# Gate and up by rows with seven block products in place of eight for part of the depth, in a two-layer trunk on one core

## The chip, the core and the metric

One Trainium2 chip, of which one core runs the program. The metric is the device time of one execution in microseconds, the median of the runs. All inputs lie in HBM when it starts, and the output is written back there.

## What is computed

Two layers on 256 tokens of width 2048, in float32. A layer is a norm, one projection that feeds eight retention heads and a gated linear recurrence, an output projection added to x, and then the part that is changed:

```
D_MODEL = 2048
SEQ = 256
DEPTH = 2
D_FF = ((8 * D_MODEL // 3 + 255) // 256) * 256
...
        x = x + mix @ w_out[l]
        h = _rmsnorm(x, norm2_g[l])
        x = x + (jax.nn.silu(h @ ffn_w_gate[l]) * (h @ ffn_w_up[l])) @ ffn_w_down[l]
    return _rmsnorm(x, final_g)
```

D_FF is 5632, which is 44 chunks of 128 columns; D_MODEL is 16 chunks.

## The kernel before, in words

Every large product is made to float32 accuracy from three products of a shorter type: a weight w is split into hi (a copy in that type, by ScalarE) and lo = w - hi (by VectorE), an activation likewise (`pair`, L122 to L134), and hi*hi, hi*lo and lo*hi are summed in PSUM.

The work is a list of units. A unit is one block of weights of up to 128x2048, which SP fetches in one DMA (`load`, L544), which is split in two halves (`split`, L568 and L569) and then used by up to four blocks of matmuls. Three raw buffers and three pairs of hi and lo buffers rotate. The main loop (L648 to L663) writes the program block by block: ahead of a unit's first and third block stands the split of half of the unit after the next; behind each block, a counter of ticks releases small pieces of other work that were put off by so many blocks. The order of the instructions on each engine comes from that loop and from a scheduler that may move them a little.

Almost all units are column units (`column_unit`, L182): the weights are stationary, the tokens move. For each of the 16 chunks of the depth, L195 multiplies the hi weights with 512 columns (256 tokens hi, 256 tokens lo), and L198 the lo weights with 256 columns. The result has features on partitions and tokens in the free dimension. Only the v part of the projection (L441 to L443) has the tokens stationary and 512 weight columns moving, three matmuls for each chunk and each half of the tokens.

The feed-forward stage of a layer goes in three parts (`THIRDS`, 15, 15 and 14 chunks of D_FF). In each, every chunk f has a gate unit and an up unit (L512 and L513), with `gate` (L501) and `up` (L506) behind them: the two halves of the PSUM tile are joined (L178, L179), scaled by the row norm of the tokens, silu is taken (L505), gate and up are multiplied (L510) and split (L126, L127). Then 16 down units add to x (L406, L407). There are 88 gate and up units in a layer, 176 in all.

Of the kernel before, what the change touches and what calls it, by code (L numbers as in the profile page):

```python
# [26 lines left out]
THIRDS = [(0, 15), (15, 15), (30, 14)]  # L27
RAW = 3
WARM = 12
# [41 lines left out]
class Unit:  # L71


    def __init__(self, src, width, blocks, done=None, begin=None):
        self.src, self.width, self.blocks = src, width, blocks
        self.done, self.begin = done, begin
        self.split_at = (0, 2)
# [3 lines left out]
def trunk(ctx: ExitStack, tc, a, out):  # L81
# [4 lines left out]
    hi_p = pool("whi", 3)  # L86
    lo_p = pool("wlo", 3)
# [3 lines left out]
    big_ps = pool("big", 4, space=bass.MemoryType.PSUM)  # L91
    sm_ps = pool("sm", 4, space=bass.MemoryType.PSUM)
# [7 lines left out]

    def small():
        return sm_ps.tile([P, 512], F32, tag="sm", name="sm_ps")
# [78 lines left out]

    def column_unit(src, n_k, operand, done, begin=None, order=None):  # L182

        u = Unit(src, n_k * P, [], begin=begin)
        order = order or list(range(n_k))

        def block(i):
            ks = order[i : i + 4]

            def run():  # L190
                if i == 0:
                    u.ps = big_ps.tile([P, 512], F32, tag="big", name="acc_ps")
                for pr in (ks[:2], ks[2:]):
                    for k in pr:
                        PE.matmul(u.ps, lhsT=u.hi[:, k * P : (k + 1) * P],  # L195
                                  rhs=operand(k).rearrange("p a t -> p (a t)"), start=k == order[0], stop=False)
                    for k in pr:
                        PE.matmul(u.ps[:, T : 2 * T], lhsT=u.lo[:, k * P : (k + 1) * P], rhs=operand(k)[:, 0, :],  # L198
                                  start=False, stop=k == order[-1])
            return run  # L200

        u.blocks += [block(i) for i in range(0, n_k, 4)]
        u.done = lambda: done(u.ps)
        return u


    def rotary(ps, name):
        z = joined_halves(ps)
        t, u, o = tmp("rt"), tmp("ru"), tmp(name)
# [7 lines left out]
    def head(l, h):  # L217
# [86 lines left out]
    def lru(l, n):  # L304
# [68 lines left out]
        def y_done(ps):  # L373
            z = joined_halves(ps)
            y = one_p.tile([P, T], F32, tag=f"gy{n}", name="y")
# [33 lines left out]
    def after_residual(k, nxt, gains):  # L409
# [3 lines left out]
        if k == KD - 1:  # L413
            tk.after(2, lambda: sums([st["xa"]], D, "rs"))
            tk.after(4, lambda: rows("rs"))
# [7 lines left out]
    def v_units(l):  # L423

        res = []
        for g in range(2):
            hold = {}
            for s in range(4):
                u = Unit(a["w_v"][l, g, s], 2048, [])

                def block(kk, u=u, s=s, hold=hold):
                    def run():
                        k = s * 4 + kk
                        if k == 0:
                            hold["ps"] = [big_ps.tile([P, 512], F32, tag="big", name="v_ps") for _ in range(2)]
                        w = slice(kk * 512, (kk + 1) * 512)
                        x2 = st["h1", k]
                        for j in range(2):
                            t = slice(j * P, (j + 1) * P)
                            ps = hold["ps"][j]  # L440
                            PE.matmul(ps, lhsT=x2[:, 0, t], rhs=u.hi[:, w], start=k == 0, stop=False)  # L441
                            PE.matmul(ps, lhsT=x2[:, 0, t], rhs=u.lo[:, w], start=False, stop=False)  # L442
                            PE.matmul(ps, lhsT=x2[:, 1, t], rhs=u.hi[:, w], start=False, stop=k == KD - 1)  # L443
# [11 lines left out]
                u.blocks = [block(kk) for kk in range(4)]  # L455
# [7 lines left out]
    def layer_units(l):  # L463
# [17 lines left out]
        for n in range(KD):  # L481
# [3 lines left out]
            u = column_unit(a["w_out"][l, n], KD, lambda k: st["mix", l, k], done, order=order)  # L485
            if n == 0:
                rest, first_done = u.blocks.pop(), u.done
                u.done = None
            if n == 1:
                def held(rest=rest, first_done=first_done):  # L490
                    rest()
                    first_done()
                u.blocks.insert(3, held)
                u.split_at = (4, 4)
            res.append(u)


        for t, (f0, nf) in enumerate(THIRDS):
            for f in range(f0, f0 + nf):
                c = {}  # L500
                def gate(ps, c=c):  # L501
                    z = joined_halves(ps)
                    c["g"] = tmp("sg")
                    V.tensor_tensor(out=z, in0=z, in1=st["rs"], op=ALU.mult)  # L504
                    S.activation(out=c["g"], in_=z, func=AF.Silu)  # L505
                def up(ps, c=c, f=f):  # L506
                    z = joined_halves(ps)
                    m = tmp("mix")
                    V.tensor_tensor(out=c["g"], in0=c["g"], in1=st["rs"], op=ALU.mult)  # L509
                    V.tensor_tensor(out=m, in0=z, in1=c["g"], op=ALU.mult)  # L510
                    st["act", f] = pair(m)
                res.append(column_unit(a["w_gate"][l, f], KD, lambda k: st["h2", k], gate))  # L512
                res.append(column_unit(a["w_up"][l, f], KD, lambda k: st["h2", k], up))  # L513
            for n in range(KD):
# [7 lines left out]
                res.append(column_unit(a[f"w_down{t}"][l, n], nf, lambda k, f0=f0: st["act", f0 + k], done))  # L522
        return res

# [19 lines left out]
    def load(n):  # L544
        if n < len(units):
            u = units[n]
            u.raw = raw_p.tile([P, 2048], F32, tag="raw", name="raw")
            pieces = 4 if n < 4 else 1
            for q in range(pieces):
                w = slice(q * u.width // pieces, (q + 1) * u.width // pieces)  # L550
                nc.sync.dma_start(out=u.raw[:, w], in_=u.src[:, w])
                if n == 0:
                    nc.sync.dma_start(out=X[:, q, :], in_=a["x"][:, q])
# [193 lines left out]
```

## Time and profile before

| | |
|---|---|
| median of 3 runs | 2257.55 us (2257.39 to 2257.93) |
| the profiled execution | 2257.48 us, its span 2255.7 us |
| busy share | PE 99%, VectorE (DVE) 67%, ScalarE (ACT) 50%, GpSimd 3% |
| moved by DMA | 422.92 MB, mean 187 GB/s |

The span runs from the first to the last instruction that the profiler saw; the profiled execution's own time is 1.8 us more. A busy share says how much of the span an engine had work in flight. For TensorE it says little about speed, since matmuls overlap: there the time from one start to the next counts.

### The profile page before, as it was taken

What the parts mean: (1) busy time and instruction counts of PE and PEld (TensorE: products, weight loads), DVE (VectorE), ACT (ScalarE), POOL (GpSimd) and SP (SyncE); (2) the same over time, 40 slices, a digit from 0 to 9 for tenths busy, and PEclk for the clock granted to TensorE, in tenths of its full rate; (3) what the DMA queues carried; (4) which work ended last, traced back from release to release, by engine and by line L of the source; (5) the groups of instructions that cost most, each with busy time, mean ns of one, the idle gap of its engine ahead of it and who ended that gap; (6) DMA issues with size and microseconds to landing.
All of it is one profiled execution on the core that took longest, in us unless ns stands there. A gap on an engine that the chain in (4) does not pass through costs nothing.

```text
span 2255.7 us, 31764 instructions
## 1 busy us (share of the span) xinstructions
PE 2239.1 (99%) x12760; PEld 1949.4 (86%) x12760; DVE 1512.5 (67%) x2405; ACT 1127.1 (50%) x1648; POOL 59.8 (3%) x97
## 2 busy tenths in 40 slices
PE   9999999999999999999999999999999999999997
PEld 7888888888888888888888888888888888888886
DVE  6888876666566655666748889766665666556665
ACT  6667544544344443444546665444443444334453
POOL 0010100000000000000000101000000000000000
PEclk9999999999999999999999999999999999999999
DMA  7555555555555555555555554555555555555553
GB/s 286 183 186 181 172 195 191 183 191 189 184 200 187 186 186 189 188 190 179 201 193 179 180 197 165 189 182 192 191 183 195 188 187 184 192 188 190 193 175 112
DMA packets 63140, 422.92 MB, mean 187 GB/s; under 512 B 7312, under 2 KB 7952, under 8 KB 24592
## 3 DMA queue, kind: packets, MB, share of 16 engines
q1 hardware_dynamic: 60912, 414.60, 52.5%
q0 software_dynamic: 1792, 5.24, 0.8%
q8 instruction: 100, 1.64, 0.3%
q10 hardware_dynamic: 288, 1.05, 0.1%
q14 instruction: 48, 0.39, 0.0%
HBM read 418.77 MB, written 2.10 MB: 187 GB/s over the span
## 4 chain that ended last, share of the span: by engine, by line
PE 97%; DVE 1%; issue 0%; DMA 0%; POOL 0%; ACT 0%; SPq 0%; DVEq 0%; POOLq 0%
PE acc_ps L195 62%; PE acc_ps L198 31%; PE v_ps L442 1%; PE v_ps L443 1%; PE v_ps L441 1%; PE sm_ps L331 1%; DVE wlo L569 0%; PE sm_ps L240 0%; DMA raw<-in_w_v_dram 0%; DVE op L130 0%; PE sm_ps L289 0%; PE sm_ps L157 0%; PE sm_ps L241 0%; PE sm_ps L256 0%; PE sm_ps L255 0%
## 5 line engine op out<-in xcount | busy, mean ns | idle before, releaser
L195 PE MATMUL acc_ps<-op,whi 128*128 128x512 f32 x6016 | 1899.8, 397 | 0.0
L198 PEld LDWEIGHTS acc_ps<-op,wlo 128*128 128x128 f32 x6016 | 1129.8, 188 | 263.4
L569 DVE TENSOR_TENSOR wlo<-raw,whi 128x1024 fp32r<-128x1024 f32 (+3 forms) x808 | 950.0, 1187 | 366.6 <-ACT whi L568 362.4
L198 PE MATMUL acc_ps<-op,wlo 128*128 128x256 f32 x6016 | 1188.6, 278 | 0.0
L568 ACT ACTIVATE whi<-raw 128x1024 fp32r<-128x1024 f32 (+3 forms) x808 | 817.3, 1029 | 657.3 <-PE acc_ps L195 578.1
L195 PEld LDWEIGHTS acc_ps<-op,whi 128*128 128x128 f32 x6016 | 920.4, 189 | 4.8 <-DVE op L127 0.7
L406 DVE TENSOR_TENSOR x<-acc_ps,x 128x256 f32<-128x256 f32 x128 | 54.2, 424 | 215.5 <-PE acc_ps L198 215.5
L126 ACT ACTIVATE op<-mix 128x256 fp32r<-128x256 f32 x104 | 43.1, 416 | 167.7 <-DVE mix L510 163.5
L505 ACT ACTIVATE sg<-z 128x256 f32<-128x256 f32 x88 | 36.8, 419 | 161.1 <-DVE z L504 161.1
L179 DVE TENSOR_TENSOR z<-acc_ps,low 128x256 f32<-128x256 f32 x256 | 106.7, 417 | 0.0
L178 ACT ACTIVATE low<-acc_ps 128x256 f32<-128x256 f32 x256 | 93.7, 366 | 0.0
L127 DVE TENSOR_TENSOR op<-mix,op 128x256 fp32r<-128x256 f32 x104 | 44.0, 424 | 42.7 <-ACT op L126 42.6
L509 DVE TENSOR_TENSOR sg<-sg,rs 128x256 f32<-128x256 f32 x88 | 37.4, 425 | 42.6 <-ACT sg L505 42.6
L407 DVE TENSOR_TENSOR x<-acc_ps,x 128x256 f32<-128x256 f32 x128 | 54.2, 424 | 4.3
L150 POOL TENSOR_TENSOR rc<-rc,mhalf 128x2 f32<-128x2 f32 x7 | 5.8, 824 | 1720.7 <-DVE rc L149 1720.7
L442 PE MATMUL v_ps<-wlo,op 128*128 128x512 f32 x128 | 50.1, 391 | 1.1 <-DVE wlo L569 1.1
L441 PE MATMUL v_ps<-whi,op 128*128 128x512 f32 x128 | 50.1, 396 | 0.5 <-ACT op L129 0.4
L443 PE MATMUL v_ps<-whi,op 128*128 128x512 f32 x128 | 50.1, 391 | 0.0
L510 DVE TENSOR_TENSOR mix<-z,sg 128x256 f32<-128x256 f32 x88 | 36.7, 417 | 0.0
L504 DVE TENSOR_TENSOR z<-z,rs 128x256 f32<-128x256 f32 x88 | 36.7, 417 | 0.0
L129 ACT ACTIVATE op<-x,par 128x256 fp32r<-128x256 f32 x64 | 31.2, 496 | 2.6 <-DMA par<-in_par_dram 1.8
L173 DVE TENSOR_TENSOR acc<-acc,sq 128x256 f32<-128x256 f32 x73 | 30.6, 420 | 1.6 <-ACT sq L172 1.0
(116 smaller groups left out, 698.9 us busy)
## 6 DMA issues: line engine op xcount, KB each, us to landing
raw<-in_w_gate_dram SPq DMA_DIRECT2D x88, 1024.0 KB, 4.8
raw<-in_w_up_dram SPq DMA_DIRECT2D x88, 1024.0 KB, 4.8
raw<-in_w_in_dram SPq DMA_DIRECT2D x80, 1024.0 KB, 4.8
raw<-in_w_down_dram SPq DMA_DIRECT2D x64, 960.0 KB, 4.7
raw<-in_w_out_dram SPq DMA_DIRECT2D x32, 1024.0 KB, 4.8
raw<-in_w_down_dram SPq DMA_DIRECT2D x32, 896.0 KB, 4.6
raw<-in_w_v_dram SPq DMA_DIRECT2D x12, 1024.0 KB, 4.8
raw<-in_w_v_dram SPq DMA_DIRECT2D x16, 256.0 KB, 6.0
```

What stands on the lines that cost most here:

```text
L127: V.tensor_tensor(out=t[:, 1, :], in0=x_ap, in1=t[:, 0, :].bitcast(F32), op=ALU.subtract)
L178: S.activation(out=low, in_=ps[:, T : 2 * T], func=AF.Copy)
L179: V.tensor_tensor(out=z, in0=ps[:, 0:T], in1=low, op=ALU.add)
L195: PE.matmul(u.ps, lhsT=u.hi[:, k * P : (k + 1) * P], rhs=operand(k).rearrange("p a t -> p (a t)"), start=k == order[0], stop=False)
L198: PE.matmul(u.ps[:, T : 2 * T], lhsT=u.lo[:, k * P : (k + 1) * P], rhs=operand(k)[:, 0, :], start=False, stop=k == order[-1])
L406: V.tensor_tensor(out=X[:, k, :], in0=ps[:, T : 2 * T], in1=X[:, k, :], op=ALU.add)
L407: V.tensor_tensor(out=X[:, k, :], in0=ps[:, 0:T], in1=X[:, k, :], op=ALU.add)
L441: PE.matmul(ps, lhsT=x2[:, 0, t], rhs=u.hi[:, w], start=k == 0, stop=False)
L442: PE.matmul(ps, lhsT=x2[:, 0, t], rhs=u.lo[:, w], start=False, stop=False)
L443: PE.matmul(ps, lhsT=x2[:, 1, t], rhs=u.hi[:, w], start=False, stop=k == KD - 1)
L568: S.activation(out=u.hi[:, w], in_=u.raw[:, w], func=AF.Copy)
L569: V.tensor_tensor(out=u.lo[:, w], in0=u.raw[:, w], in1=u.hi[:, w].bitcast(F32), op=ALU.subtract)
```

## The change

Gate and up are made in slabs of four chunks f (`SLAB`), 22 in all, by a new function `slab_units`. The tokens are stationary now, as in v: each matmul multiplies 128 tokens with 512 weight columns (four chunks of 128). The parts of the feed-forward stage become 16, 16 and 12 chunks. A slab has eight units, one for each pair p of depth chunks; a unit fetches the gate and the up weights of its pair for four chunks f, in two DMAs.

For a pair there are two halves of the tokens, two depth chunks and two outputs (gate, up), so eight products of 128x128 by 128x512, each of three matmuls. In the last five pairs these eight are made, in four PSUM banks (products 2, 4, 3 and 8 in the code). In the first three pairs (`FAST`) they are made by seven, with sums and differences of the blocks: `combined` makes four of them from the tokens, once for a layer, behind the output projection; `up_parts`, `first_sums` and `second_sums` make the ones of the weights, for each slab anew, in place in the raw buffer, and split them. So a pair of the first three has four prepared halves of 1024 columns (one of them 512) in place of two. The seven products use seven banks, all eight are taken in a slab; `shared` joins four of them on VectorE, `gate` and `up` add the result to the other four, and the four 128x512 results of a slab are transposed by TensorE (`columns`) and split as before (`operands_of`). The norm of the tokens is now a column of scalars (`rsc`), so the row form of it is no longer made for this stage.

The hi and lo buffers become six halves of 1024 columns each (`HALVES`), and `prepare`, called ahead of every block, writes up to two halves' preparation as soon as a block that frees a buffer has been written. PSUM banks are numbered and given out by role. `hold` puts the last block of the first column units of a group behind those of the next, as before was done for the output projection alone.

```
-THIRDS = [(0, 15), (15, 15), (30, 14)]
+THIRDS = [(0, 16), (16, 16), (32, 12)]
+SLAB = 4
+FAST = 3
 RAW = 3
+HALVES = 6
...
-    hi_p = pool("whi", 3)
-    lo_p = pool("wlo", 3)
...
+    def half_tiles(u, h):
+        u.hi[h] = hi_p.tile([P, 1024], F32R, tag="whi", name="whi")
+        u.lo[h] = lo_p.tile([P, 1024], F32R, tag="wlo", name="wlo")
+        return u.hi[h], u.lo[h]
+
+    def parts(hi, lo, raw):
+        S.activation(out=hi, in_=raw, func=AF.Copy)
+        V.tensor_tensor(out=lo, in0=raw, in1=hi.bitcast(F32), op=ALU.subtract)
+
+    def plain_halves(u, width):
+        def prep(h):
+            w = width // 2
+            hi, lo = half_tiles(u, h)
+            parts(hi[:, :w], lo[:, :w], u.raw[:, h * w : (h + 1) * w])
+        u.preps = [lambda: prep(0), lambda: prep(1)]
+
...
-            tk.after(4, lambda: rows("rs"))
+            if nxt == "h1":
+                tk.after(4, lambda: rows("rs"))
+        if nxt == "h2" and k % 2 and k < 2 * FAST:
+            tk.after(3, lambda: combined(k // 2, gains))
+
+    def combined(p, gains):
+
+        r = one_p.tile([P, 4, T], F32, tag="rot4", name="asum")
+        for i in range(2):
+            S.activation(out=r[:, i, :], in_=X[:, 2 * p + i, :], func=AF.Copy, scale=gains(2 * p + i))
+        a11, a21, a12, a22 = (r[:, i, j * P : (j + 1) * P] for i in range(2) for j in range(2))
+        f = r[:, 2:4, :].rearrange("p a (b t) -> p (a b) t", b=2)
+        V.tensor_tensor(out=f[:, 0, :], in0=a21, in1=a22, op=ALU.add)
+        V.tensor_tensor(out=f[:, 1, :], in0=f[:, 0, :], in1=a11, op=ALU.subtract)
+        V.tensor_tensor(out=f[:, 2, :], in0=a11, in1=a21, op=ALU.subtract)
+        V.tensor_tensor(out=f[:, 3, :], in0=a12, in1=f[:, 1, :], op=ALU.subtract)
...
+        S.activation(out=t[:, :, 0, :], in_=f, func=AF.Copy)
+        V.tensor_tensor(out=t[:, :, 1, :], in0=f, in1=t[:, :, 0, :].bitcast(F32), op=ALU.subtract)
...
-            for f in range(f0, f0 + nf):
-                c = {}
-                def gate(ps, c=c):
-                    z = joined_halves(ps)
-                    c["g"] = tmp("sg")
-                    V.tensor_tensor(out=z, in0=z, in1=st["rs"], op=ALU.mult)
-                    S.activation(out=c["g"], in_=z, func=AF.Silu)
-                def up(ps, c=c, f=f):
-                    z = joined_halves(ps)
-                    m = tmp("mix")
-                    V.tensor_tensor(out=c["g"], in0=c["g"], in1=st["rs"], op=ALU.mult)
-                    V.tensor_tensor(out=m, in0=z, in1=c["g"], op=ALU.mult)
-                    st["act", f] = pair(m)
-                res.append(column_unit(a["w_gate"][l, f], KD, lambda k: st["h2", k], gate))
-                res.append(column_unit(a["w_up"][l, f], KD, lambda k: st["h2", k], up))
...
+            for f in range(f0, f0 + nf, SLAB):
+                res += slab_units(l, f, f == f0)
+            res[-1].done = columns_again
+            first = len(res)
...
+        def product(i, x, w, go, end):
+
+            if i not in c:
+                c[i] = bank(c["ids"][i], "row_ps")
+                go = True
+            ps = c[i]
+            PE.matmul(ps, lhsT=x[0], rhs=w[0], start=go, stop=False)
+            PE.matmul(ps, lhsT=x[0], rhs=w[1], start=False, stop=False)
+            PE.matmul(ps, lhsT=x[1], rhs=w[0], start=False, stop=end)
...
+        def loader(p):
+            def load(raw):
+                for i, name in enumerate(("w_gate", "w_up")):
+                    src = a[name][l, f0 : f0 + SLAB, :, 2 * p * P : (2 * p + 2) * P]
+                    nc.sync.dma_start(out=raw[:, i * 1024 : (i + 1) * 1024].rearrange("p (f w) -> p f w", f=SLAB),
+                                      in_=src.rearrange("f p w -> p f w"))
+            return load
+
+        def piece(t, k):
+            return t.rearrange("p (f k w) -> p f k w", f=SLAB, k=2)[:, :, k, :]
+
+        for p in range(KD // 2):
+            u = Unit(loader(p))
+            plain = p >= FAST
+            if not plain:
+                def gate_parts(u=u):
+                    hi, lo = half_tiles(u, 0)
+                    parts(hi, lo, u.raw[:, 0:1024])
+
+                def up_parts(u=u):
+                    hi, lo = half_tiles(u, 1)
+                    flat = lambda t: t[:, 0:512].rearrange("p (f w) -> p f w", f=SLAB)
+                    parts(flat(hi), flat(lo), piece(u.raw[:, 1024:2048], 1))
+                    r = u.raw.rearrange("p (c f k w) -> p c f k w", c=2, f=SLAB, k=2)
+                    V.tensor_tensor(out=r[:, :, :, 0, :], in0=r[:, 1].rearrange("p f k w -> p k f w"),
+                                    in1=r[:, :, :, 0, :], op=ALU.subtract)
+
+                def first_sums(u=u):
+                    g, p_ = u.raw[:, 0:1024], u.raw[:, 1024:2048]
+                    V.tensor_tensor(out=piece(p_, 1), in0=piece(p_, 1), in1=piece(g, 0), op=ALU.subtract)
+                    V.tensor_tensor(out=piece(g, 1), in0=piece(g, 1), in1=piece(p_, 1), op=ALU.subtract)
+                    hi, lo = half_tiles(u, 2)
+                    parts(hi, lo, g)
+
+                def second_sums(u=u):
+                    hi, lo = half_tiles(u, 3)
+                    parts(hi, lo, u.raw[:, 1024:2048])
...
+                        x = {1: lambda: block_of(0, 2 * p), 2: lambda: block_of(0, 2 * p + 1),
+                             4: lambda: block_of(1, 2 * p + 1), 3: lambda: form(3), 5: lambda: form(0),
+                             6: lambda: form(1), 7: lambda: form(2)}
+                        w = {1: (0, 0), 2: (0, 1), 5: (2, 0), 4: (2, 1), 7: (3, 0), 6: (3, 1)}
...
+                for todo, frees in (((1, 2), [0]), ((3, 5), [1]), ((4, 7), [2]), ((6,), [3])):
+                    u.add(run(todo), frees)
...
+                plain_halves(u, 2048)
+                for j, side, i in ((0, 0, 2), (1, 0, 4), (0, 1, 3), (1, 1, 8)):
+                    def go(j=j, side=side, i=i, p=p, u=u):
+                        for k in range(2):
+                            product(i, block_of(j, 2 * p + k), (piece(u.hi[side], k), piece(u.lo[side], k)),
+                                    False, p == KD // 2 - 1 and k == 1)
+                        if p == KD // 2 - 1:
+                            tk.after(1, {2: lambda: gate(0), 4: lambda: gate(1), 3: lambda: up(0), 8: lambda: up(1)}[i])
+                    u.add(go, [side] if j else [])
...
+            S.activation(out=m1, in_=c[1], func=AF.Copy)
+            S.activation(out=m5, in_=c[5], func=AF.Copy)
+            V.tensor_tensor(out=u2, in0=c[6], in1=m1, op=ALU.add)
+            V.tensor_tensor(out=u3, in0=c[7], in1=u2, op=ALU.add)
+            V.tensor_tensor(out=u2, in0=u2, in1=m5, op=ALU.add)
+            V.tensor_tensor(out=m5, in0=m5, in1=u3, op=ALU.add)
+
+        def gate(j):
+            t, i = ((c["a"][:, 0, :], 2), (c["b"][:, 1, :], 4))[j]
+            V.tensor_tensor(out=t, in0=c[i], in1=t, op=ALU.add)
+            S.activation(out=t, in_=t, func=AF.Silu, scale=st["rsc"][:, j : j + 1])
+
+        def up(j):
+            g = (c["a"][:, 0, :], c["b"][:, 1, :])[j]
+            t, i = ((c["b"][:, 0, :], 3), (c["a"][:, 1, :], 8))[j]
+            V.tensor_tensor(out=t, in0=c[i], in1=t, op=ALU.add)
+            V.scalar_tensor_tensor(out=t, in0=t, scalar=st["rsc"][:, j : j + 1], in1=g, op0=ALU.mult, op1=ALU.mult)
+            c["act", j] = t
+            if j == 1:
+                tk.after(1, lambda: columns(0))
+
+        def columns(i):
+            ps = small()
+            for f in range(2):
+                for j in range(2):
+                    at = (2 * f + j) * P
+                    PE.transpose(ps[:, at : at + P], c["act", j][:, (2 * i + f) * P : (2 * i + f + 1) * P], ident)
+            tk.after(1, lambda: operands_of(i, ps))
+
+        def operands_of(i, ps):
+            for f in range(2):
+                st["act", f0 + 2 * i + f] = pair(ps[:, f * T : (f + 1) * T])
+            if i == 0:
+                tk.after(1, lambda: columns(1))
...
+    def prepare(most):
+
+        for _ in range(most):
+            i = at["next"]
+            if i >= len(items) or i - HALVES >= at["free"]:
+                return
+            n, u, h = items[i]
+            u.preps[h]()
+            if h == len(u.preps) - 1:
+                load(n + RAW)
```

Where VectorE's instructions stood in a gate and an up unit, before (wlo is the lo half of weights, z the joined PSUM halves, sg silu of the gate, mix the product, op its split):

```order
L569 TENSOR_TENSOR wlo_5043<-raw_4918,whi_5042 128x1024
L179 TENSOR_TENSOR z_5036<-acc_ps_4998,low_5035 128x256
L569 TENSOR_TENSOR wlo_5043<-raw_4918,whi_5042 128x1024
L504 TENSOR_TENSOR z_5036<-z_5036,rs_3941 128x256
L509 TENSOR_TENSOR sg_5039<-sg_5039,rs_3941 128x256
L569 TENSOR_TENSOR wlo_5094<-raw_4966,whi_5093 128x1024
L179 TENSOR_TENSOR z_5084<-acc_ps_5046,low_5083 128x256
L569 TENSOR_TENSOR wlo_5094<-raw_4966,whi_5093 128x1024
L510 TENSOR_TENSOR mix_5087<-z_5084,sg_5039 128x256
L127 TENSOR_TENSOR op_5090<-mix_5087,op_5090 128x256
```

These ten are all that VectorE had in two units. In the change, VectorE at the border of two slabs, from the last PSUM read of one (L719, `up`) into the next one's second pair (raw_4905; L144 splits the transposed results of the slab that ended):

```order
L719 TENSOR_TENSOR ca_4870<-row_ps_4894,ca_4870 128x512
L720 SCALAR_TENSOR_TENSOR cb_4871<-cb_4871,rc_4045,ca_4870 128x512
L720 SCALAR_TENSOR_TENSOR ca_4870<-ca_4870,rc_4045,cb_4871 128x512
L206 TENSOR_TENSOR wlo_5050<-raw_4905,whi_5049 128x512
L648 TENSOR_TENSOR raw_4905<-raw_4905 128x8x128
L144 TENSOR_TENSOR op_5081<-sm_ps_5062,op_5081 128x256
L653 TENSOR_TENSOR raw_4905<-raw_4905 128x4x128
L144 TENSOR_TENSOR op_5084<-sm_ps_5062,op_5084 128x256
L654 TENSOR_TENSOR raw_4905<-raw_4905 128x4x128
L206 TENSOR_TENSOR wlo_5070<-raw_4905,whi_5069 128x1024
L206 TENSOR_TENSOR wlo_5088<-raw_4905,whi_5087 128x1024
```

And on, in its third pair (raw_4940; L648, L653 and L654 are the sums made of the weights):

```order
L206 TENSOR_TENSOR wlo_5108<-raw_4940,whi_5107 128x1024
L144 TENSOR_TENSOR op_5115<-sm_ps_5102,op_5115 128x256
L206 TENSOR_TENSOR wlo_5122<-raw_4940,whi_5121 128x512
L144 TENSOR_TENSOR op_5118<-sm_ps_5102,op_5118 128x256
L648 TENSOR_TENSOR raw_4940<-raw_4940 128x8x128
L653 TENSOR_TENSOR raw_4940<-raw_4940 128x4x128
L654 TENSOR_TENSOR raw_4940<-raw_4940 128x4x128
L206 TENSOR_TENSOR wlo_5135<-raw_4940,whi_5134 128x1024
```

What was spread evenly is now dense here: between the reads of L719 and the third pair's wlo_5135 stand 18 instructions, and those of L653, L654 and the hi copies behind them follow from one another.

TensorE in that third pair (whi_5121, whi_5134 and whi_5144 are the hi parts of its second, third and fourth half):

```order
L616 MATMUL row_ps_5073<-whi_5121,s2_3528 128x512
L617 MATMUL row_ps_5073<-wlo_5122,s2_3528 128x512
L618 MATMUL row_ps_5073<-whi_5121,s2_3528 128x512
L616 MATMUL row_ps_5077<-whi_5134,s2_3528 128x512
L616 MATMUL row_ps_5094<-whi_5134,op_3483 128x512
L616 MATMUL row_ps_5098<-whi_5144,s2_3528 128x512
L616 MATMUL row_ps_5111<-whi_5144,s2_3528 128x512
L617 MATMUL row_ps_5077<-wlo_5135,s2_3528 128x512
L618 MATMUL row_ps_5077<-whi_5134,s2_3528 128x512
L617 MATMUL row_ps_5094<-wlo_5135,op_3483 128x512
L618 MATMUL row_ps_5094<-whi_5134,op_3483 128x512
```

The hi products of the third and fourth half were moved ahead of the lo products; the first of them needs whi_5134, which ScalarE copies when L654 of this pair is done.

## Rows read from the trace of the kernel before

**Rows 1.** The page: busy time by engine, and the chain that ended last.

```profile
PE 2239.1 (99%) x12760; PEld 1949.4 (86%) x12760; DVE 1512.5 (67%) x2405; ACT 1127.1 (50%) x1648; POOL 59.8 (3%) x97
...
PE 97%; DVE 1%; issue 0%; DMA 0%; POOL 0%; ACT 0%; SPq 0%; DVEq 0%; POOLq 0%
```

**Rows 2.** Timeline of TensorE in a gate unit: start, us, engine, line, operation, count.

```profile
1000.48 0.63 PE L195 MATMUL acc_ps<-op,whi 128*128 128x512 f32 x2
...
1008.14 0.62 PE L195 MATMUL acc_ps<-op,whi 128*128 128x512 f32 x2
```

**Rows 3.** Timeline of TensorE in the v units.

```profile
14.71 0.50 PE L442 MATMUL v_ps<-wlo,op 128*128 128x512 f32 x1 [0.60 <-DVE wlo L569]
15.05 0.40 PE L443 MATMUL v_ps<-whi,op 128*128 128x512 f32 x1
...
18.96 0.39 PE L442 MATMUL v_ps<-wlo,op 128*128 128x512 f32 x1
...
21.68 0.39 PE L443 MATMUL v_ps<-whi,op 128*128 128x512 f32 x1
```

**Rows 4.** Timeline of TensorE around two transposes of a head.

```profile
170.82 0.38 PE L289 MATMUL sm_ps<-ident,on 128*128 128x128 f32 x2
170.96 0.71 PE L195 MATMUL acc_ps<-op,whi 128*128 128x512 f32 x2
```

**Rows 5.** Busy time by engine in stretches of w_out, down, and gate and up: length; PE, PEld, DVE, ACT, POOL; clock, DMA.

```profile
280.00:360.00 80.00, 80.00 (x467) 70.09 (x466) 60.02 (x103) 37.80 (x56) 4.91 (x6) 1.00 0.55 190
...
700.00:780.00 80.00, 80.00 (x461) 69.79 (x461) 49.34 (x73) 38.20 (x57) 0.00 (x0) 1.00 0.54 186
900.00:1000.00 100.00, 100.00 (x576) 87.27 (x575) 61.76 (x90) 48.56 (x72) 0.00 (x0) 1.00 0.54 189
```

**Rows 6.** Groups by line and shape: busy us, mean ns, idle before.

```profile
L569 DVE TENSOR_TENSOR wlo<-raw,whi 128x1024 fp32r<-128x1024 f32 x600 | 726.6, 1219 | 329.4 <-ACT whi L568 327.6
L568 ACT ACTIVATE whi<-raw 128x1024 fp32r<-128x1024 f32 x600 | 626.6, 1055 | 413.7 <-PE acc_ps L195 367.8 <-PE v_ps L443 24.1 <-issue 10.6
L130 DVE SCALAR_TENSOR_TENSOR op<-x,par,op 128x256 fp32r<-128x256 f32 x64 | 30.4, 477 | 0.6 <-ACT op L129 0.6
L569 DVE TENSOR_TENSOR wlo<-raw,whi 128x512 fp32r<-128x512 f32 x16 | 10.8, 684 | 3.4 <-ACT whi L568 3.3
L673 DVE TENSOR_TENSOR x<-x,sm_ps 128x768 f32<-128x768 f32 x4 | 3.5, 949 | 2.0 <-ACT rs L670 2.0
```

**Rows 7.** Timeline of VectorE and ScalarE in a gate unit.

```profile
1003.28 1.06 ACT L568 ACTIVATE whi<-raw 128x1024 fp32r<-128x1024 f32 x1 [1.00 <-PE acc_ps L195]
...
1004.37 1.22 DVE L569 TENSOR_TENSOR wlo<-raw,whi 128x1024 fp32r<-128x1024 f32 x1 [1.64 <-ACT whi L568]
...
1005.52 0.42 DVE L179 TENSOR_TENSOR z<-acc_ps,low 128x256 f32<-128x256 f32 x1
...
1005.85 1.22 DVE L569 TENSOR_TENSOR wlo<-raw,whi 128x1024 fp32r<-128x1024 f32 x1
...
1006.98 0.41 DVE L510 TENSOR_TENSOR mix<-z,sg 128x256 f32<-128x256 f32 x1
```

**Rows 8.** DMA: issues by source, KB each, us to landing.

```profile
raw<-in_w_gate_dram SPq DMA_DIRECT2D x88, 1024.0 KB, 4.8
...
x<-in_x_dram SPq DMA_DIRECT2D x4, 128.0 KB, 5.7
```

**Rows 9.** Timeline of the first matmuls of the program.

```profile
1.04 5.49 PE L614 MATMUL sm_ps<-ones 128*128 128x128 f32 x24 [1.04 <-DVE sp L584]
...
7.25 0.39 PE L442 MATMUL v_ps<-wlo,op 128*128 128x512 f32 x1
7.47 0.39 PE L443 MATMUL v_ps<-whi,op 128*128 128x512 f32 x1
```

**Rows 10.** Busy time by stretch at the end (columns as in rows 5).

```profile
2242.00:2244.00 2.00, 0.57 (x5) 0.33 (x3) 1.27 (x3) 0.09 (x1) 0.00 (x0) 1.00 0.00 0
...
2246.00:2248.00 2.00, 0.26 (x3) 0.07 (x1) 1.28 (x2) 0.38 (x1) 1.24 (x2) 0.58 0.00 0
```

More of the change, by code (lines that the diff above doesn't have):

```diff
@@ L71, with __init__, add @@
 class Unit:
[L74 to L77, printed above, removed]
+    def __init__(self, load, begin=None, done=None, preps=()):
+        self.load, self.begin, self.done = load, begin, done
+        self.preps = list(preps)
+        self.blocks = []
+        self.hi, self.lo = {}, {}
+    def add(self, fn, frees=()):
+        self.blocks.append((fn, [(self, h) for h in frees]))
 @with_exitstack
@@ L453, in evacuate @@
                         )
-                u.blocks = [block(kk) for kk in range(4)]
+                for kk in range(4):
+                    u.add(block(kk), [kk // 2] if kk % 2 else [])
                 if s == 3:
@@ L525, in last_sums, with columns_again @@
+    def columns_again():
+        free, later = st["free"], st["later"]
+        turn["big"] = free[:3] + later[:1]
+        turn["small"] = free[3:] + later[1:]
     def last_sums():
@@ L547, in load @@
             u.raw = raw_p.tile([P, 2048], F32, tag="raw", name="raw")
[L548 to L553, printed above, removed]
-                    if q == 0:
-                        nc.sync.dma_start(out=par, in_=a["par"])
+            if n < 4:
+                for q in range(4):
+                    u.load(u.raw, slice(q * 512, (q + 1) * 512))
+                    if n == 0:
+                        nc.sync.dma_start(out=X[:, q, :], in_=a["x"][:, q])
+                        if q == 0:
+                            nc.sync.dma_start(out=par, in_=a["par"])
+            else:
+                u.load(u.raw)
             if n < 3:
@@ L558, in load, with quarter @@
                 nc.sync.dma_start(out=X[:, k, :], in_=a["x"][:, k])
[L560 to L562 removed]
+    def quarter(n, q):
         u = units[n]
[L564 to L570 removed]
+        if q % 2 == 0:
+            half_tiles(u, q // 2)
+        w = slice(q % 2 * 512, (q % 2 + 1) * 512)
+        parts(u.hi[q // 2][:, w], u.lo[q // 2][:, w], u.raw[:, q * 512 : (q + 1) * 512])
+        if q == 3:
             load(n + RAW)
@@ L621, in operands @@
     def operands(n, q):
-        split(n, q, 4)
+        quarter(n, q)
         k = 4 * n + q
@@ L646, in trunk @@
         tk.after(30 + i, part)
+    items = [(n, u, h) for n, u in enumerate(units) for h in range(len(u.preps))]
+    where = {(id(u), h): i for i, (n, u, h) in enumerate(items)}
+    free = [False] * len(items)
+    at = {"next": 8, "free": 0}
+    def prepare(most):
[7 more added lines that the diff above has]
+                load(n + RAW)
+            at["next"] += 1
     for n, u in enumerate(units):
@@ L650, in trunk @@
             u.begin()
-        for b, block in enumerate(u.blocks):
+        for b, (block, frees) in enumerate(u.blocks):
             if n < 3:
@@ L654, in trunk @@
             else:
-                for part in range(2):
-                    if b == u.split_at[part]:
-                        if n == 3:
-                            split(4, part)
-                        split(n + 2, part)
+                prepare(2)
             block()
+            for v, h in frees:
+                free[where[id(v), h]] = True
+            while at["free"] < len(items) and free[at["free"]]:
+                at["free"] += 1
             tk.tick()
```

140 lines of the change are left out of this document (100 added, 40 removed).

## The prediction, made before the change was run

> **What bounds the kernel now.** I read the page first: PE is busy for 99% of the span, and the chain that ended last runs over PE for 97% [rows 1]. So a microsecond of matmul pace counts, and VectorE's 67% and ScalarE's 50% count only where they make PE wait. Then the timeline for the pace. In a gate unit a pair of depth chunks begins every (1008.14 - 1000.48) / 11 = 0.696 us [rows 2], which is 0.348 us a chunk and 16 x 0.348 = 5.57 us a unit. In the v units, the only place with tokens stationary, twelve matmuls of 512 columns take 21.68 - 18.96 = 2.72 us, 0.227 us each [rows 3]. The stretch view says how even the rest is: in gate and up VectorE is busy 61.8 us of 100, in w_out 60.0 of 80, in down 49.3 of 80, and the granted clock is 1.00 everywhere [rows 5].
>
> **What TensorE saves.** Out go 176 units at 5.57 us: 980.3 us. In come, for a slab, three pairs with seven products and five with eight, 61 products or 183 matmuls of 512 columns: 183 x 0.227 = 41.5 us. Its eight transposes go in two groups of four; two take 170.96 - 170.82 = 0.14 us [rows 4], four 0.28, a slab 0.56. For 22 slabs that is 913.9 + 12.3 = 926.2 us. The row form of the norm falls away in each layer, four short matmuls of about 0.11 us: 0.9 us in all. PE's own work falls by 980.3 - 926.2 + 0.9 = 55 us. A slab is 42.1 us of PE where eight units were 44.6.
>
> **What VectorE takes on.** An instruction of 1024 elements takes 1.22 us and one of 512 takes 0.68 [rows 6]. If the next one is ready, it starts before the end: 1005.85 to 1006.98 is 1.13 us for 1024, 1005.52 to 1005.85 is 0.33 for 256 [rows 7], so I hold VectorE for 1.13, 0.60 and 0.33. One that needs the one before starts some 0.03 behind its end, as the lo half does behind its hi half (1003.28 + 1.06 = 1004.34, start 1004.37) [rows 7]. A first pair needs three lo halves of 1024 and one of 512, one sum of 1024 and two of 512: 4 x 1.13 + 3 x 0.60 = 6.3 us, against 21 x 0.227 = 4.8 us of PE. A plain pair needs 2.3 us against 24 x 0.227 = 5.4. With four joins, two gates, four steps of up and four splits (10 x 0.60 + 4 x 0.33 = 7.3) a slab makes 3 x 6.3 + 5 x 2.3 + 7.3 = 37.7 us of VectorE in 42.1 us of PE. On average it fits. But only six halves can be ready ahead, one and a half of the first pairs, so the surplus of the plain pairs can't be saved up for the dense part. That place decides.
>
> **The dense part, step by step.** The order at the border of two slabs, above, is walked from the end of the last product of a slab, with holds in us. The read of L719 0.60; two multiplies of L720, 0.65 each (a multiply by a scalar column of 256 took 0.477 where plain ones took 0.42 [rows 6, 7], so 0.05 on top): 1.90. Second pair: lo of 512 0.60, sum of 1024 1.13, split 0.33, sum 0.60, split 0.33, sum to its end 0.68: 5.57. The hi copy by ScalarE needs that sum: 1.055 [rows 6] and twice 0.03: 6.69. Two lo halves 2.26, and the first of the third pair 1.13: 10.08. Split 0.33, lo of 512 0.60, split 0.33: 11.34. The three sums, now each behind the last: 1.25, 0.71, 0.68: 13.98. The hi copy 1.11: 15.1 us. Only then can TensorE start product 5 of the third pair. By its own work it would be there after 51 matmuls and eight transposes: 51 x 0.227 + 0.56 = 12.1. So it waits 3.0 us. Two hi products later (0.45 us) it needs the fourth half's hi copy, which ScalarE ends about 0.95 us after the third's: 0.5 us more. That is 3.5 us in a slab, and nothing hides it, because behind that place the plain pairs are TensorE's own (they free the buffers one by one).
>
> This holds for 18 slabs. Four open a part behind down units, where VectorE has no reads of up, multiplies and splits of an earlier slab ahead of it: 1.90 + 4 x 0.33 = 3.2 us less, so about 1.0 us is left, the two half microseconds around the hi copies. The waits are 18 x 3.5 + 4 x 1.0 = 67 us. Each end of a wait costs a little more: behind the wait at 14.71 the next matmul starts 0.34 us later and not 0.227 [rows 3], 0.11 x 44 = 4.8 us.
>
> **Parts with no price of their own.** `combined` adds to VectorE at most 4 x 0.42 + 0.68 = 2.4 us in w_out, three times a layer; VectorE is idle there for 20 us in 80 [rows 5], and without that cover it would be 6 x 2.4 = 14 us. The same depth of down units is only cut otherwise. Six halves in place of three whole buffers give column units half a unit more lead; the wait for a buffer stays ScalarE's. The rotation of the banks lets a slab's first blocks use banks that were read long before. The DMAs carry the same bytes, but in runs of 1 KB for each partition where there were 8 KB. A unit of 8 KB runs landed in 4.8 us, and 128 KB in 1 KB runs in 5.7 us in the crowd of the start [rows 8]. The closest call is the sixth unit of a slab, fetched when the third pair is prepared: TensorE then has two plain pairs ahead of it, 10.9 us, of which landing, a hi and a lo copy take 4.8 + 1.1 + 1.2 = 7.1, so 3 us of lateness cost nothing. I take 0; the upper end, 1 us a slab beyond that, is 22 us.
>
> **Sums of the weights in strides.** L648, L653 and L654 read and write runs of 128 out of 256; no row has that form. The nearest, L673, reads a 128x768 form with a repeated row in 0.949 us [rows 6], on the line of 1024 in 1.22 and 512 in 0.68, so I take the plain price. The lower bound is the same (a stride gives nothing back). The upper I set at a quarter more on these three, 5.3 us twice in the dense part: about +1.2 us a slab, 26 us.
>
> **The sum.** Against the profiled execution's own time, 2257.48, which is the median within 0.1 us: 2257.5 - 55.0 + 67 + 4.8 = 2274.3. I forecast **2274 us**, slower by 0.7%. A measurement of this kernel can tell about 0.2%, 4.5 us, from no change.
>
> **Rivals.**
>
> *The cover holds.* If the dense part were 3.5 us shorter, PE would stay the bound: 2257.5 - 55 = 2202 to 2207. For it: 37.7 us of VectorE fit into 42.1. Against it: the order is fixed, each price above is that of a row, and the two copies by ScalarE lie between the sums and nothing else is written there. The sides change when the dense part shrinks by 0.8 us (17 us over 22 slabs), 5% of 15.1. I give 0.14, with a part of it near no change.
>
> *Strided sums cost more.* At a quarter more the time is 2274 + 26 = 2300, at twice the price over 2370. 0.11.
>
> *The clock falls in the waits.* At the end of the span TensorE has 0.57 us of work in two, and soon after the granted clock goes to 0.58 in a stretch [rows 10], on its way to the lower of its two levels, 1.2 GHz. At the start 24 short matmuls ran from 1.04 for 5.49 us, 0.23 each, before matmuls came at the full pace of 0.22 for 512 columns [rows 9]. If every long wait brought that back, some 5.5 us of work at half pace would lose 2.8 us, 18 x 2.8 = 50 us: 2324. Against it: the waits lie between stretches without a gap, and the end's gaps were separated by little work. The Trainium skill, in TensorE: Matmul & The Clock Gate (HAM oscillation), says that a wait inside a loop can throttle the engine each time round; the trace before has no such wait in its middle, and does not decide it. 0.07.
>
> *The moving operand is slower in strides.* 58 of the 61 products of a slab move weights in four runs of 128. No row has it; in v the columns are contiguous. A tenth more on the 132 matmuls of a slab that lie outside the dense part is 132 x 0.023 x 22 = 66 us: 2340. The Trainium skill, in Advanced Engine Details and Errata (Memory Cachelines), says that any access that is not contiguous slows matmuls significantly; it stands there under PSUM, which is written contiguously here, so it need not hold for this operand. 0.06.
>
> **Chances.** The forecast's own case has 0.62: of it 0.53 slower by over 0.2%, 0.06 within it, 0.03 faster. Of the 0.14 where the cover holds, 0.11 is faster and 0.03 within. The other three, 0.24, are slower. Together: faster 0.14, same 0.09, slower 0.77. The forecast's own range is 2258 to 2295. For eight in ten I go from 2246, into the part of the first rival, to 2312, over the dearer sums; outside are the full cover and the clock.
>
> **What would show it.** In the profile after: the gate and up stretches with a slab every 45.5 to 46 us (42 if the cover holds); PE's share at about 97%, its wait for whi of 2 to 3.5 us once a slab, in the third pair, released by ScalarE's hi copy, and that copy released by L654. VectorE near 85% in these stretches, with waits for whi of about 1.1 us three times a slab. L648 at 1.22 us and L653 at 0.68 if strides are free. The row matmuls 0.227 us apart outside the waits. I am wrong if TensorE doesn't wait there, if it waits for DMA in the plain pairs, or if the granted clock is below 1.00 in the middle.

## The result, and the profile after

| | before | after |
|---|---|---|
| median of 4 runs | 2257.74 us (2257.39 to 2258.31) | 2311.13 us (2311.08 to 2311.37) |
| busy share of PE, VectorE, ScalarE | 99, 67, 50% | 97, 77, 53% |
| mean granted clock of TensorE | 0.998 | 0.985 |

The change is slower by a factor of 1.0236, interval 1.0219 to 1.0254: 53.4 us. The sign of the prediction holds, the size does not, since 16.8 us were forecast. The time lies inside the range of 2246 to 2312, but that is luck: the upper end was set for dearer sums, which did not come, and a falling clock, which did, was put outside it. The page after, to be laid beside [rows 1]: TensorE has 1438 matmuls fewer, and VectorE 266 us more of work.

```profile
PE 2232.6 (97%) x11322; PEld 1872.9 (81%) x11322; DVE 1778.7 (77%) x2545; ACT 1223.6 (53%) x1620; POOL 47.6 (2%) x97
```

The list of waits, longest in total first, names the place (engine, waiting tile and line, releaser, us in total, times, longest):

```profile
...
ACT whi L205 <- DVE raw L654: 141.5, 66, 4.2
...
PEld row_ps L616 <- ACT whi L205: 78.4, 48, 3.2
...
PE row_ps L616 <- ACT whi L205: 57.4, 45, 2.8
...
ACT whi L205 <- DMA raw<-in_w_gate_dram: 36.3, 37, 3.1
ACT whi L205 <- DMA raw<-in_w_up_dram: 29.1, 44, 2.0
```

TensorE waits for the hi copy, the hi copy for L654, as forecast. ScalarE waits for DMA too, but none of that reaches TensorE: in the plain pairs its row matmuls at the upper clock have no gap over 0.1 us beyond their pace. The wait itself, in the timeline of a slab that began at 988.56 (VectorE and ScalarE first, then TensorE, each in order of time):

```profile
988.93 0.68 DVE L719 TENSOR_TENSOR ca<-row_ps,ca 128x512 f32<-128x512 f32 x1
...
993.85 0.69 DVE L654 TENSOR_TENSOR raw<-raw 128x512 f32<-128x512 f32 x1
995.73 3.50 DVE L206 TENSOR_TENSOR wlo<-raw,whi 128x1024 fp32r<-128x1024 f32 x3 [1.19 <-ACT whi L205]
...
1000.40 1.22 DVE L648 TENSOR_TENSOR raw<-raw 128x1024 f32<-128x1024 f32 x1
1001.66 0.69 DVE L653 TENSOR_TENSOR raw<-raw 128x512 f32<-128x512 f32 x1
1002.38 0.69 DVE L654 TENSOR_TENSOR raw<-raw 128x512 f32<-128x512 f32 x1
...
1003.11 5.80 ACT L205 ACTIVATE whi<-raw 128x1024 fp32r<-128x1024 f32 x6 [2.38 <-DVE raw L654]
```

```profile
1000.81 0.40 PE L617 MATMUL row_ps<-wlo,s 128*128 128x512 f32 x1
1001.04 0.40 PE L618 MATMUL row_ps<-whi,s 128*128 128x512 f32 x1
1004.22 0.50 PE L616 MATMUL row_ps<-whi,s 128*128 128x512 f32 x1 [2.78 <-ACT whi L205]
1004.55 0.40 PE L616 MATMUL row_ps<-whi,op 128*128 128x512 f32 x1
1005.17 1.22 PE L616 MATMUL row_ps<-whi,s 128*128 128x512 f32 x2 [0.22 <-ACT whi L205]
1006.19 0.63 PE L617 MATMUL row_ps<-wlo,s 128*128 128x512 f32 x1
1006.61 0.63 PE L618 MATMUL row_ps<-whi,s 128*128 128x512 f32 x1
1007.04 0.63 PE L617 MATMUL row_ps<-wlo,op 128*128 128x512 f32 x1
...
1008.88 0.40 PE L617 MATMUL row_ps<-wlo,s 128*128 128x512 f32 x1
1009.11 0.40 PE L618 MATMUL row_ps<-whi,s 128*128 128x512 f32 x1
```

Up to the wait, matmuls start 0.23 us apart, behind it 0.42 to 0.43, and from 1008.88 again 0.23. The stretch view shows why; its columns are as in [rows 5], the clock the third from the right:

```profile
988.50:1036.30 47.80, 44.80 (x192) 35.69 (x192) 39.12 (x46) 24.93 (x30) 0.00 (x0) 0.96 0.54 176
999.00:1004.00 5.00, 2.44 (x11) 1.59 (x9) 4.01 (x7) 1.88 (x3) 0.00 (x0) 1.00 0.65 210
1004.00:1008.40 4.40, 3.96 (x10) 2.85 (x11) 4.20 (x4) 4.40 (x6) 0.00 (x0) 0.63 0.13 41
1008.40:1036.00 27.60, 27.60 (x123) 22.84 (x122) 21.30 (x23) 13.33 (x15) 0.00 (x0) 1.00 0.73 237
```

The granted clock fell behind the wait, to the lower of its two levels (1.2 GHz in place of 2.4): a mean of 0.63 over 4.4 us. Before, it was 1.00 in gate and up [rows 5]; 700:780 there is gate and up as well and not down, whose units in that part ran from 556.9 to 640.6. After, it falls 17 times in the middle of the span. The slabs sort by it. 16 idle 2.75 to 2.80 us in this wait: all have a fall and last 47.5 to 47.8 us. The first slab of each layer idles 2.30: no fall and 45.8 us in layer one, a fall and 47.2 in layer two. The four that open a part behind down idle 0.75 to 1.04 there: no fall, 43.1 to 43.4 us.

### The profile page after: what moved, and what is told of

It reads as the page before. It is cut to its first block, busy times and chain, and to the rows that moved or that the text cites. A ratio compares the mean times of both kernels' runs of the same rounds, so it can differ in the third digit from the quotient of the medians.

```text
span 2309.3 us, 29771 instructions
## 1 busy us (share of the span) xinstructions
PE 2232.6 (97%) x11322; PEld 1872.9 (81%) x11322; DVE 1778.7 (77%) x2545; ACT 1223.6 (53%) x1620; POOL 47.6 (2%) x97
## 3 DMA queue, kind: packets, MB, share of 16 engines
q1 hardware_dynamic: 221424, 414.61, 53.6%
## 4 chain that ended last, share of the span: by engine, by line
PE 78%; DVE 12%; issue 3%; ACT 3%; DMA 2%; POOL 0%; SPq 0%; ACTq 0%; DVEq 0%; POOLq 0%
PE acc_ps L233 30%; PE acc_ps L236 15%; PE row_ps L616 9%; PE row_ps L617 9%; PE row_ps L618 9%; DVE wlo L206 5%; ACT whi L205 3%; DMA raw<-in_w_up_dram 2%; DVE raw L648 2%; PE acc_ps L524 1%; PE acc_ps L525 1%; PE acc_ps L523 1%; DVE raw L654 1%; DVE raw L653 1%; DVE op L144 1%
## 5 line engine op out<-in xcount | busy, mean ns | idle before, releaser
L205 ACT ACTIVATE whi<-raw 128x1024 fp32r<-128x1024 f32 (+2 forms) x940 | 926.5, 1006 | 895.0 <-PE acc_ps L233 435.2
L206 DVE TENSOR_TENSOR wlo<-raw,whi 128x1024 fp32r<-128x1024 f32 (+2 forms) x940 | 1073.1, 1157 | 384.2 <-ACT whi L205 378.5
L233 PE MATMUL acc_ps<-op,whi 128*128 128x512 f32 x3200 | 1014.0, 398 | 0.0
L236 PEld LDWEIGHTS acc_ps<-op,wlo 128*128 128x128 f32 x3200 | 600.7, 188 | 140.8
L236 PE MATMUL acc_ps<-op,wlo 128*128 128x256 f32 x3200 | 630.3, 278 | 0.0
L233 PEld LDWEIGHTS acc_ps<-op,whi 128*128 128x128 f32 x3200 | 490.0, 189 | 1.6
L617 PE MATMUL row_ps<-wlo,op 128*128 128x512 f32 x1078 | 425.3, 395 | 0.0
L616 PE MATMUL row_ps<-whi,op 128*128 128x512 f32 x1078 | 424.2, 394 | 0.0
L618 PE MATMUL row_ps<-whi,op 128*128 128x512 f32 x1078 | 423.8, 393 | 0.0
L618 PEld LDWEIGHTS row_ps<-whi,op 128*128 128x128 f32 x1078 | 204.8, 190 | 42.2
L616 PEld LDWEIGHTS row_ps<-whi,op 128*128 128x128 f32 x1078 | 204.8, 190 | 42.2
L616 PE MATMUL row_ps<-whi,s 128*128 128x512 f32 x264 | 113.0, 445 | 57.4 <-ACT whi L205 57.4
L618 PE MATMUL row_ps<-whi,s 128*128 128x512 f32 x264 | 108.8, 412 | 0.0
L648 DVE TENSOR_TENSOR raw<-raw 128x1024 f32<-128x1024 f32 x66 | 80.6, 1221 | 0.8
```

What stands on the lines that cost most here:

```text
L205: S.activation(out=hi, in_=raw, func=AF.Copy)
L206: V.tensor_tensor(out=lo, in0=raw, in1=hi.bitcast(F32), op=ALU.subtract)
L233: PE.matmul(u.ps, lhsT=u.hi[side(k)][:, col_of(k)], rhs=operand(k).rearrange("p a t -> p (a t)"), start=k == order[0], stop=False)
L236: PE.matmul(u.ps[:, T : 2 * T], lhsT=u.lo[side(k)][:, col_of(k)], rhs=operand(k)[:, 0, :], start=False, stop=k == order[-1])
L616: PE.matmul(ps, lhsT=x[0], rhs=w[0], start=go, stop=False)
L617: PE.matmul(ps, lhsT=x[0], rhs=w[1], start=False, stop=False)
```

## Experiments

The theory: the dense part on VectorE makes TensorE wait some 3 us in a slab, and that wait also lowers the clock. The rivals: TensorE's rows are dearer than taken (strided operand, transposes, DMA), or VectorE is too busy on the whole.

**Two and one fast pairs in place of three.** The third pair, where the wait is, becomes plain; TensorE has more to do.

```
-FAST = 3
+FAST = 2     (and +FAST = 1)
```

> Two of eight pairs by seven products (FAST = 2), all else as in the change. Theory (VectorE's dense stretch of three first pairs in a row sets the wait in the third pair, and that wait lowers the clock): without a third pair the wait is gone, the granted clock is 1.00 in gate and up. Three more matmuls a slab, 22 x 3 x 0.227 = 15 us, on top of the change's own matmul work, which by its trace is 49 us under the kernel before: 2257.7 - 49 + 15 + up to 10 of small waits = 2224 to 2234 us. Rival (what is lost lies in the row form itself: transfers in 1 KB runs, weights moving in strides): the loss of some 100 us stays nearly whole, about 2300 us.

> One of eight pairs by seven products (FAST = 1). Theory: no wait, clock 1.00, and again 15 us more of matmuls than with two: 2239 to 2249 us. Rival (row form itself): about 2300 us or more.

With two: 2230.27 us (2229.48 to 2230.79), 0.9876 of before [0.9861, 0.9891]; with one 2244.31 in a single run. Both lie where the theory has them. With two, TensorE has 66 matmuls more than in the change and ends 81 us earlier, its share is 99% and the clock's mean 0.998 again. So seven products for eight pay on TensorE, and the third such pair in a row is what costs. This doesn't yet part the wait from the clock.

**The wait filled.** Ten matmuls that nobody reads, into a bank not yet in use, stand in TensorE's order where it waits. They leave the wait's end where it was, since VectorE and ScalarE don't depend on them; only TensorE isn't idle.

```
+                            if p == FAST - 1 and i == 5:
+                                spare = bank(c["ids"][8], "fill_ps")
+                                for _ in range(10):
+                                    PE.matmul(spare, lhsT=x[1]()[0], rhs=u.hi[1][:, 0:512], start=True, stop=True)
```

> The change with ten spare matmuls of 512 columns in each slab, written to a bank that is unused at that time, ahead of product 5 of the third pair; what they give is not used. They take 10 x 0.227 = 2.3 us of the 2.95 us wait, which itself stays as long as it was. Theory (the clock falls because TensorE has nothing to do in that wait): the clock stays at 1.00 and the time falls by the 28 us that the low stretches cost in the change's trace, to 2281 to 2290 us. Rival (the clock falls for another reason, the stationary tokens or the strided weights): the clock still falls once a slab, 2309 us or more.

2288.24 us (2287.68 to 2289.00), ratio 1.0133 [1.0118, 1.0149]: 22.9 us less than the change, with 220 matmuls more. TensorE's timeline at the wait:

```profile
993.84 2.43 PE L678 MATMUL fill_ps<-whi,op 128*128 128x512 f32 x10
996.79 0.50 PE L616 MATMUL row_ps<-whi,s 128*128 128x512 f32 x1 [0.51 <-ACT whi L205]
...
998.30 0.39 PE L617 MATMUL row_ps<-wlo,s 128*128 128x512 f32 x1
998.53 0.39 PE L618 MATMUL row_ps<-whi,s 128*128 128x512 f32 x1
```

Behind it the pace stays 0.23, and there is no fall in the middle of the span. A slab takes 46.25 us in place of 47.76: a fall costs 1.5 us, 17 of them 25.5. In the four slabs whose wait was only 1 us the ten matmuls are too many and cost 0.8 each, 3 us in all; 25.5 - 3 = 22.5, beside the 22.9 measured. The clock's part is shown.

**The fast pairs spread out.** The same instructions in another order: plain pairs stand between the fast ones, so that VectorE's dense part is broken up.

```
-        for p in range(KD // 2):
+        for p in (0, 3, 1, 4, 2, 5, 6, 7):
```

> The change with the pairs of a slab taken in the order 0, 3, 1, 4, 2, 5, 6, 7, so that a plain pair stands behind each of the first three; the same instructions, no work added or left out. Theory (the sums are dear only because three pairs with four halves each stand in a row): the waits of 75 us shrink to under 10, the clock stays at 1.00, 2257.7 - 49 + 5 to 15 = 2212 to 2224 us. Rival (VectorE has too much work in a slab on the whole, with its waits for ScalarE): the wait only moves, 2260 us or more.

2219.52 us (2218.97 to 2219.63), ratio 0.9829 [0.9813, 0.9845]. VectorE has the same work as in the change, within 5 us, and its share is even higher; TensorE is at 99%. Its page:

```profile
PE 2194.9 (99%) x11322; PEld 1861.5 (84%) x11322; DVE 1774.4 (80%) x2545; ACT 1213.0 (55%) x1620; POOL 47.6 (2%) x97
```

The group whose first matmul waited, in the change and then here (busy us, mean ns, idle before):

```profile
L616 PE MATMUL row_ps<-whi,s 128*128 128x512 f32 x264 | 113.0, 445 | 57.4 <-ACT whi L205 57.4
```

```profile
L616 PE MATMUL row_ps<-whi,s 128*128 128x512 f32 x264 | 103.4, 392 | 0.0
```

The wait is gone, and the clock with it (0.998). That VectorE is too busy on the whole falls as a theory: it was busy at the wrong time.

**The wait halved, in two ways.** First from VectorE's side: L653 and L654 fall away in the third pair, so this kernel leaves out two sums of the weights.

```
-                def first_sums(u=u):
+                def first_sums(u=u, p=p):
...
+                    if p < FAST - 1:
```

> The change without the two sums of 512 (L653 and L654) in the third pair of each slab; those sums of the weights are left out of the computation. Theory (these two stand in the chain that ends the wait): the chain is 1.4 us shorter in 18 slabs, the wait about 1.5 us in place of 2.95, 25 to 30 us less. If a wait of that length still lowers the clock: 2281 to 2286 us; if it does not, the 23 us that the spare matmuls gave back come on top: 2258 to 2265 us. Rival (the wait ends by something else, a transfer or a buffer): 2305 us or more.

Then from TensorE's: five spare matmuls in place of ten.

```
-                                for _ in range(10):
+                                for _ in range(5):
```

> As with ten spare matmuls, but five: 1.1 us of the wait is filled and about 1.8 us stay idle. Theory: the length of the slab without the clock's fall is the same as with ten; 2283 to 2290 us if an idle 1.8 us leaves the clock at 1.00, about 2306 to 2311 us if it does not. Either outcome says how short a wait is harmless; it does not speak against the theory.

Without the sums: 2255.91 us in a single run, slightly under the 2258 expected; of the 16 slabs, which now idle 1.29 to 1.34 us, the clock fell in one. With five spare matmuls: 2308.05 in a single run; the 16 idle 1.57 to 1.66, and it fell in 14. TensorE behind the wait in each, first without the sums:

```profile
1024.39 0.40 PE L618 MATMUL row_ps<-whi,s 128*128 128x512 f32 x1
1026.11 0.50 PE L616 MATMUL row_ps<-whi,s 128*128 128x512 f32 x1 [1.33 <-ACT whi L205]
...
1027.63 0.40 PE L617 MATMUL row_ps<-wlo,s 128*128 128x512 f32 x1
1027.86 0.39 PE L618 MATMUL row_ps<-whi,s 128*128 128x512 f32 x1
```

```profile
1053.09 0.50 PE L616 MATMUL row_ps<-whi,s 128*128 128x512 f32 x1 [1.63 <-ACT whi L205]
...
1054.61 0.63 PE L617 MATMUL row_ps<-wlo,s 128*128 128x512 f32 x1
1055.04 0.63 PE L618 MATMUL row_ps<-whi,s 128*128 128x512 f32 x1
```

In the five-matmul kernel a slab with a fall takes 47.8 us, one without 46.26: the same 1.5 us. The clock is therefore no separate trouble beside the wait; its falls become rare when less of the wait stays idle. Where exactly they end these runs don't settle.

**Three tries at a better order.** A second order of the pairs:

```
+        for p in (0, 3, 4, 1, 5, 2, 6, 7):
```

> The spread order in another form, pairs 0, 3, 4, 1, 5, 2, 6, 7: two plain pairs behind the first one, where VectorE still has the reads and splits of the slab before. Theory (VectorE is late there by what the earlier slab left to it): the small waits for the transposes and in the second pair shrink, 2212 to 2220 us against 2219.5 of the first spread order. Rival (the rest is the transposes themselves): the same within 2 us.

> The second spread order once more, with rounds, for an interval: 2216 to 2219 us.

And with it the transposes of a slab's results one block later, in `up`:

```
-                tk.after(1, lambda: columns(0))
+                tk.after(2, lambda: columns(0))
```

> The second spread order (0, 3, 4, 1, 5, 2, 6, 7), and the transposes of a slab one block of matmuls later. In the change's trace each of their two groups holds TensorE up for about 0.5 us, where I had reckoned 0.28. Theory (in the first group part of that is a wait for VectorE's multiply, L720): one block later the multiply is done, 0.2 to 0.4 us less in 22 slabs, 2208 to 2213 us against 2217.3 of the second spread order. Rival (the transposes themselves cost that): 2215 to 2219 us.

The second order: 2217.29 us in a single run, and in four runs 2217.78 (2216.13 to 2218.42), 0.9820 [0.9803, 0.9836], which is 1.7 us below the first order. Its trace has 4.5 us less at the transposes and 2.6 us more in gaps below 0.1 us between the row matmuls. With the later transposes 2214.08 us (2213.27 to 2214.62), 0.9805 [0.9791, 0.9820]: between the two expectations, 3.7 us below the same order without them. In the first spread order TensorE waited for L720 ahead of its transposes (list of waits):

```profile
PEld sm_ps L730 <- DVE cb L720: 8.5, 14, 1.3
...
PEld sm_ps L730 <- DVE ca L720: 4.6, 16, 0.3
```

The second order alone has 2.8 us (4 times) for cb and 1.1 (4 times) for ca. The last kernel has 1.0 (4 times) for ca, and for cb this:

```profile
PEld sm_ps L730 <- DVE cb L720: 1.8, 2, 0.9
```

So the second order had already removed most of that wait, and the later transposes took only 1 us of the rest. The two traces lie 4.3 us apart: 0.7 us at the transposes, 2.3 in gaps below 0.1 us between the row matmuls, 1.3 outside the slabs. That the multiply was what held TensorE up is not shown by this run.

This is the fastest version found, 43.7 us under before.

## Why the prediction was wrong in size

**What held.** The walk of the dense part. It put the end of the second pair's L654 5.57 us behind the last product, the next lo half at 6.69, L648 of the third pair at 11.34, the end of the sums at 13.98 and TensorE's start at 15.1. Counted from 988.93, where L719 takes that product, the rows above have 994.54 - 988.93 = 5.61, 6.80, 11.47, 1003.07 - 988.93 = 14.14 and 15.29. The wait is 2.95 us over the pace (1004.22 - 1001.04 - 0.23) with 0.38 to 0.39 two matmuls later and 0.11 behind each, where 3.0, 0.5 and 0.11 were forecast. All gaps over 0.1 us beyond the pace, at the upper clock and away from the transposes, are 77 in the 22 slabs and make 69 us; forecast were 67 + 4.8.

The strided sums cost the plain price, as the groups by shape say (1.22 and 0.68 were taken), so that rival falls:

```profile
L648 DVE TENSOR_TENSOR raw<-raw 128x1024 f32<-128x1024 f32 x66 | 80.6, 1221 | 0.8
...
L654 DVE TENSOR_TENSOR raw<-raw 128x512 f32<-128x512 f32 x66 | 45.6, 690 | 1.7
L653 DVE TENSOR_TENSOR raw<-raw 128x512 f32<-128x512 f32 x66 | 45.4, 688 | 1.4
```

VectorE is busy 39.1 of 47.8 us in a slab, 82%. The DMAs of 1 KB runs landed in 4.2 us (gate) and 5.5 (up), and TensorE waits for nothing behind them, as taken. One row was misread: 49.3 us of 80 were taken for VectorE in down, but that stretch is gate and up [rows 5]; no term of the sum rests on it.

**The step that failed first: the sum carries no term for the clock.** It added 18 waits of 3.5 us and kept TensorE at its upper level behind each, and the clock below 1.00 in the middle is a sign of being wrong by its own words. The prediction had the case as a rival with a chance of 0.07, "against it: the waits lie between stretches without a gap". That reason was worthless: dense work on both sides of a wait of 2.95 us did not keep the clock up, it fell in all 16 such slabs. [Rows 10], where it falls at the end, was the sign in the trace before, and was set aside. The rival's price was too high, 50 us: it cost about 25, 17 falls of 1.5 us and not 18 of 2.8. The Trainium skill, in TensorE: Matmul & The Clock Gate (HAM oscillation), says that a wait inside a loop can throttle the engine each time round; the trace after agrees, with 17 falls.

**The step that failed second: "PE's own work falls by 55 us".** The trace after measures this term. From the first matmul of gate and up in each part to the first one of down, TensorE took 982.7 us before and 1029.1 after. Without the 69 us of gaps above and the 27 us by which the matmuls in the 17 stretches of lower clock exceed the pace of 0.227, 933.0 us are left. All the rest of the span took 1272.9 us before and 1280.2 after. TensorE's own work fell by 982.7 - 933.0 - 7.3 = 42.4 us, 12.6 short. The timeline after shows most of that at the transposes:

```profile
992.30 0.39 PE L618 MATMUL row_ps<-whi,op 128*128 128x512 f32 x1
...
993.66 0.39 PE L618 MATMUL row_ps<-whi,s 128*128 128x512 f32 x1
993.88 0.39 PE L616 MATMUL row_ps<-whi,op 128*128 128x512 f32 x1
994.11 0.27 PE L730 MATMUL sm_ps<-ident,cb 128*128 128x128 f32 x1
...
994.44 0.27 PE L730 MATMUL sm_ps<-ident,ca 128*128 128x128 f32 x1
994.47 0.48 PE L617 MATMUL row_ps<-wlo,op 128*128 128x512 f32 x1
994.78 0.40 PE L618 MATMUL row_ps<-whi,op 128*128 128x512 f32 x1
```

From 992.30 six matmuls take 993.66 - 992.30 = 1.36 us, 0.227 each, as forecast: weights in runs of 128 move no slower. The Trainium skill's sentence that access which is not contiguous slows matmuls significantly (Advanced Engine Details and Errata, Memory Cachelines; it stands under PSUM) doesn't show for this operand. But around four transposes the two gaps are 994.47 - 993.88 = 0.59 and 994.78 - 994.47 = 0.31 us, 0.45 more than two paces, where [rows 4] had given 0.28. The slab's other group takes 0.55, part of it a wait for L720. Together 1.00 for 0.56, 7 us over the 16 slabs that have both groups among row matmuls. The transposes of the other six stand among down's matmuls and cost 0.7 us a slab, 1 us more than taken. Two transposes were read from a place where the next matmul's start ended the count, and the slower matmul behind them was left out. Another 2 us are gaps below 0.1 us between the row matmuls, and about 3 us lie outside gate and up and these transposes; where is not known.

The spread order, 38 us under before, isn't quite this term. Its clock stays up and no gap over 0.1 us is left between its row matmuls but at the transposes. There TensorE waits longer for L720 than in the change: the 48 gaps at transposes in its slabs come to 17.1 us beyond the pace, those of the change to 11.8. The list of waits of the change, to be laid beside that of the spread order above:

```profile
PEld sm_ps L730 <- DVE ca L720: 4.8, 16, 0.3
...
PEld sm_ps L730 <- DVE cb L720: 3.4, 16, 0.2
```

**The sum, corrected.** Forecast: -55 + 71.8 + 0 = +16.8. Measured in the trace after: -42.4 (own work) + 69 (gaps) + 27 (matmuls at the lower clock) = +53.6, which is also the difference of the two spans, 2309.3 - 2255.7. These are parts of one trace, so that they add up says nothing of causes. The causes rest on the runs: the filled wait gave back 22.9 us, about 26 without its cost in four slabs, for the clock, and the spread order 91.6 us for waits and clock together, beside 96 less the 5 us that it waits longer at the transposes.

## What to carry to other kernels

When a change moves work from the engine that bounds to one with room, walk the other engine's order at its densest place, in us, and not its mean share: here 82%, with the dense part in the wrong place, took some 90 us longer than the same instructions spread out. Price a recurring wait of TensorE twice, once for its length and once for the slower matmuls behind it. Filling the wait with idle matmuls tells the two apart cheaply, and here reordering removed both.

## What the runs showed of the hardware that was not expected

Short waits lowered TensorE's clock even between long stretches of dense matmuls. By the idle time in the wait: 2.75 to 2.80 us, a fall in 16 of 16 slabs; 2.30, in 1 of 2; 1.57 to 1.66, in 14 of 16; 1.29 to 1.34, in 1 of 16; 0.75 to 1.15, in none of 8; about 0.5, in none of 16. The order isn't quite by length: at 2.30 one of the two slabs had no fall. A fall made matmuls of 512 columns start 0.43 us apart in place of 0.227 and cost 1.5 us of the slab, as much with part of the wait filled as without.
